# Probabilities times values for four query blocks per value matmul, with one probability tile per query block

## The chip, the cores and the metric

The kernel runs on one core of a Trainium2 chip. The metric is the time of one execution on the device, in microseconds (us). A kernel is timed by runs of the whole program, and its figure is the median of them. A profile is one further execution, recorded by the hardware; its own time and its span (first to last instruction) are given with it.

## The reference, cut to what matters

Two layers of a decoder trunk are computed for 1024 tokens with 16 learned tokens ahead of them. Each layer has three attention branches side by side: a forgetting attention (FoX, 8 heads of 64), a latent attention (MLA, 8 heads, 96 wide for the scores and 64 for the values) and a sliding-window attention. The first two are causal over the whole sequence, and their inner part is the one that the change touches:

```python
def block(args):                      # one block of 128 queries, all heads
    i, qi = args[0], args[1]
    s = jnp.einsum('bqhd,bkhd->bhqk', qi, k).astype(jnp.float32) * scale
    if log_cum is not None:           # FoX only: s += log_cum[query] - log_cum[key]
        ...
    mask = (kpos[None, :] <= qpos[:, None]) & key_ok[None, :]
    s = jnp.where(mask, s, NEG)
    p = jax.nn.softmax(s, axis=-1)
    return jnp.einsum('bhqk,bkhd->bqhd', p.astype(v.dtype), v)
```

All of it is in float32. Each branch is then gated, projected, merged with the other two through sigmoid gates, projected again and added to the layer's input.

## The kernel before, in words

**Precision.** A float32 product is made of fp32r matmuls: an operand is split into a high part and a low part, and high times high, high times low and low times high are added in PSUM. In `mm3` (lines 171 to 178) this is three matmuls of a projection (lines 175, 176, 177). In the values product it is done otherwise: the two parts of the values stand side by side as the 128 stationary columns of one weight tile (64 high, 64 low), so one weight tile meets the high part of the probabilities (line 310) and then the low part (line 312).

**Attention of one head.** The 16 learned tokens are a small block of their own; the 1024 tokens are 8 query blocks and 8 key blocks of 128. `softmax_of` makes the scores of one query block for all keys that it sees (144 columns for block 0, 1040 for block 7) in chunks of up to 512 columns (lines 802, 804 for FoX, line 1001 for MLA), VectorE adds the mask and takes the running minimum from PSUM into the probability tile `P` (line 255), ScalarE takes the exponential in place and the row sum (line 260), and GpSimd copies the 16 columns of the learned tokens out to `pmeta` (line 298). `P` is 1040 columns wide and comes from a ring of 5 buffers in FoX and 6 in MLA, `NP = (5, 6)`.

**Probabilities times values.** The probabilities must be turned so that keys lie on the partitions. `flipped` (lines 264 to 272) transposes up to four 128x128 blocks on TensorE into one PSUM tile `ps_t` (line 268), ScalarE copies the high part to `pth` (line 157), VectorE subtracts to get the low part `ptl` (line 158). `attention` works in groups of four query blocks with one PSUM tile `o` of 512 columns, but inside a group in two halves (`sub`) of two query blocks. Each half makes its two softmaxes, then walks the key blocks in pairs: a flip holds two key blocks for two query blocks (512 columns; on the diagonal three blocks, 384 columns), and each key block gets two matmuls (lines 310, 312) of 256 columns, or of 128 for the last key block on the diagonal. Then `halves` adds the two halves of the partitions of `o` into `u` (lines 280, 281), and the second half of the group begins. One head has 10 flips, 36 transposes and 40 values matmuls; there are 32 heads in all (2 layers, 2 branches, 8 heads).

**Values.** `load_v` (lines 393 to 402) fetches the values of a pair of heads with one DMA into `vraw`, which takes a buffer of the `P` ring, and GpSimd rounds them and subtracts (lines 391, 401) to fill `vp` (2 buffers).

**What orders the work.** The program is written against a scheduler that sets the order of every engine's instructions when the kernel is built: earlier in the program goes first, and what is not ready, by its model of time, is passed over by later work. Each buffer, and each PSUM bank, is guarded by semaphores as a whole. After every group `fill()` puts dense projections behind it as written in `PLAN` (gates, `z` columns, and in MLA columns of the first branch's projection), and through that the dense matmuls and the attention are mixed on TensorE. All DMAs are issued by SyncE (SP) from one queue, in order.

## Time and profile before

| | |
|---|---|
| median of 3 runs | 2570.98 us (2567.51 to 2572.38) |
| the profiled execution, its own time | 2569.85 us |
| its span, first to last instruction | 2567.8 us |
| granted TensorE clock, mean | 0.998 |
| VectorE busy | 1273.4 us (50%) |
| ScalarE busy | 1205.8 us (47%) |
| GpSimd busy | 1012.9 us (39%) |
| DMA, queue 1: packet time as a share of 16 engines' span | 38.0% |

In the rows of the profile PE is TensorE's matmul, PEld its weight load, DVE VectorE, ACT ScalarE, POOL GpSimd and SP SyncE. A row names the line, the engine, the operation, the output and its inputs by the program's names, and the shapes. [...] The stages of layer 0 lie in this order: FoX attention from about 300 to 600 us, the window attention to about 825, MLA to about 1090, then the merge; in layer 1 FoX from about 1580 to 1910, MLA from about 2090 to 2360.

### The profile page before, as it was taken

The page shows a single profiled execution, that of the slowest core. Times are in us where ns is not written, and L with a number is a line of the kernel's source. Part 1 is how long each engine was busy: PE and PEld are TensorE (multiplying, and loading weights), DVE is VectorE, ACT ScalarE, POOL GpSimd, SP SyncE. Part 2 cuts the span into 40 slices and gives each one's busy share as a digit, 9 for nine tenths or more (in the row PEclk, how much of TensorE's full clock was granted, in tenths as well). Part 3 has the DMA queues.
Part 4 walks back from the last instruction along what each step waited for, and adds up shares of the span by engine and source line. Part 5 has one row for each costly group of instructions (what it writes and reads, how often), then busy time and mean ns, then how long its engine had stood idle before and what let it go on. Part 6 is the DMA issues. An engine that isn't in the chain of part 4 may idle for free.

```text
span 2567.8 us, 42092 instructions
## 1 busy us (share of the span) xinstructions
PE 2517.1 (98%) x15446; PEld 2247.5 (88%) x15446; DVE 1273.4 (50%) x3279; ACT 1205.8 (47%) x2704; POOL 1012.9 (39%) x990
## 2 busy tenths in 40 slices
PE   8999999999999999999999999999999999999998
PEld 7999899999888999899998888888887888887797
DVE  6454355544363445657156463545434623565643
ACT  5234355545374556654233343555435634566433
POOL 2241545443332424463523325454423342353644
PEclk9999999999999999999999999999999999999999
DMA  5244512222634434364333353221326362453532
GB/s 170 62 136 150 189 54 82 73 78 77 172 105 115 129 101 126 102 228 166 114 90 99 97 198 138 66 88 56 98 69 176 100 169 81 124 146 115 183 130 74
DMA packets 137630, 303.39 MB, mean 118 GB/s; under 512 B 22560, under 2 KB 63296, under 8 KB 137424
## 3 DMA queue, kind: packets, MB, share of 16 engines
q1 hardware_dynamic: 137424, 300.71, 38.0%
q8 instruction: 122, 2.00, 0.3%
q14 instruction: 84, 0.69, 0.1%
HBM read 211.98 MB, written 88.66 MB: 117 GB/s over the span
## 4 chain that ended last, share of the span: by engine, by line
PE 79%; DMA 5%; DVE 2%; ACT 2%; POOL 2%; issue 1%; SPq 0%; POOLq 0%; ACTq 0%; DVEq 0%
PE ps_pj L175 14%; PE ps_pj L176 14%; PE ps_pj L177 14%; PE ps_t L268 5%; PE ps_s L1001 3%; PE ps_o L312 3%; PE ps_o L310 2%; PE ps_s L177 2%; PE ps_s L176 2%; PE ps_s L175 2%; PE ps_s L804 1%; PE ps_s L802 1%; PE ps_o L176 1%; PE ps_o L177 1%; PE ps_o L175 1%
## 5 line engine op out<-in xcount | busy, mean ns | idle before, releaser
L158 POOL TENSOR_TENSOR wl<-wr,wh 128x1024 fp32r<-128x1024 f32 (+1 forms) x156 | 376.1, 2411 | 776.7 <-ACT wh L157 653.5
L175 PE MATMUL ps_pj<-hh,wh 128*128 128x512 f32 (+1 forms) x1920 | 672.7, 350 | 3.5 <-ACT gt L657 2.0
L176 PE MATMUL ps_pj<-hl,wh 128*128 128x512 f32 (+1 forms) x1920 | 671.0, 349 | 0.0
L177 PE MATMUL ps_pj<-hh,wl 128*128 128x512 f32 (+1 forms) x1920 | 669.6, 349 | 0.9 <-POOL wl L158 0.9
L175 PEld LDWEIGHTS ps_pj<-hh,wh 128*128 128x128 f32 x1920 | 361.3, 188 | 46.7 <-ACT gt L657 2.6
L177 PEld LDWEIGHTS ps_pj<-hh,wl 128*128 128x128 f32 x1920 | 361.5, 188 | 42.3 <-POOL wl L158 1.1
L176 PEld LDWEIGHTS ps_pj<-hl,wh 128*128 128x128 f32 x1920 | 361.4, 188 | 39.4 <-issue 0.5
L158 DVE TENSOR_TENSOR ptl<-ps_t,pth 128x512 fp32r<-128x512 f32 (+1 forms) x386 | 244.5, 640 | 143.6 <-ACT pth L157 137.8
L260 ACT ACTIVATE P<-P,mn 128x656 f32<-128x656 f32 (+8 forms) x272 | 207.0, 761 | 165.1 <-DVE mn L255 160.5
L157 ACT CAST pth<-ps_t 128x512 fp32r<-128x512 f32 (+1 forms) x386 | 205.7, 546 | 165.3 <-PE ps_t L268 131.9
L157 ACT CAST wh<-wr 128x1024 fp32r<-128x1024 f32 (+1 forms) x156 | 162.1, 1039 | 237.0 <-PE ps_pj L176 134.5
L268 PE MATMUL ps_t<-ident,P 128*128 128x128 f32 x1152 | 186.2, 275 | 0.8 <-DVE ptl L158 0.7
L310 PE MATMUL ps_o<-pth,vp 128*128 128x256 f32 (+1 forms) x640 | 167.2, 277 | 2.7 <-DVE u L281 1.7
L312 PE MATMUL ps_o<-ptl,vp 128*128 128x256 f32 (+1 forms) x640 | 159.4, 287 | 2.7 <-DVE ptl L158 2.5
L298 POOL COPY pmeta<-P 128x16 f32<-128x16 f32 x256 | 49.3, 196 | 270.1 <-ACT P L260 261.9
L1001 PE MATMUL ps_s<-kt,qt 96*128 96x328 f32 (+9 forms) x696 | 146.4, 327 | 2.7 <-DVE mn L255 2.6
L268 PEld LDWEIGHTS ps_t<-ident,P 128*128 128x128 f32 x1152 | 134.2, 140 | 8.6 <-DVE ptl L158 1.5
L310 PEld LDWEIGHTS ps_o<-pth,vp 128*128 128x128 f32 x640 | 120.6, 189 | 11.2 <-ACT pth L157 1.7
L809 POOL TENSOR_TENSOR cm<-ckb,tri 128x128 f32<-128x128 f32 (+1 forms) x136 | 60.3, 445 | 175.2 <-DVE mn L255 171.4
L312 PEld LDWEIGHTS ps_o<-ptl,vp 128*128 128x128 f32 x640 | 120.6, 188 | 9.6 <-DVE ptl L158 5.6
L281 DVE TENSOR_TENSOR u<-ps_o,hv 64x256 f32<-64x256 f32 x128 | 53.9, 421 | 135.4 <-ACT hv L280 120.2
L1001 PEld LDWEIGHTS ps_s<-kt,qt 96*128 96x128 f32 (+1 forms) x696 | 108.0, 186 | 10.1 <-DVE mn L255 5.2
(354 smaller groups left out, 5641.7 us busy)
## 6 DMA issues: line engine op xcount, KB each, us to landing
wr<-in_w_dram SPq DMA_DIRECT2D x108, 512.0 KB
gate_d<-gt SPq DMA_DIRECT2D x72, 256.0 KB
gt<-gate_d SPq DMA_DIRECT2D x24, 520.0 KB
wr<-in_wbr_dram SPq DMA_DIRECT2D x24, 512.0 KB
gt<-gate_d SPq DMA_DIRECT2D x24, 512.0 KB
kn_d<-sg SPq DMA_DIRECT2D x16, 520.0 KB
ckb<-ck_d SPq DMA_DIRECT2D x16, 520.0 KB
kt<-kn_d SPq DMA_DIRECT2D x16, 520.0 KB
```

What stands on the lines that cost most here:

```text
L157: nc.scalar.copy(hi, src)
L158: (eng or nc.vector).tensor_tensor(lo, src, _f(hi), ALU.subtract)
L175: nc.tensor.matmul(dst, w1, rh[:, k, c0:c1], start=(k == 0), stop=False)
L176: nc.tensor.matmul(dst, w1, rl[:, k, c0:c1], start=False, stop=False)
L177: nc.tensor.matmul(dst, wl[:, k * P:k * P + m], rh[:, k, c0:c1], start=False, stop=(k == nk - 1))
L260: nc.scalar.activation(s[:rows, :n], s[:rows, :n], AF.Exp, bias=prev, scale=-1.0, accum_out=total)
L268: nc.tensor.transpose(t[:kk, c:c + rows], src, ident[:rows, :rows])
L281: nc.vector.tensor_tensor(u[mine, :n], o[mine, :n], t[mine, :n], ALU.add)
L310: nc.tensor.matmul(dst, vp[:, j + x, vs], ph[:, cols], start=(j + x == 0), stop=False)
L312: nc.tensor.matmul(dst, vp[:, j + x, vs], pl[:, cols], start=False, stop=(diag and x == 1))
L809: nc.gpsimd.tensor_tensor(cm[:rows, :rows], ckb[:rows, d:n], tri[:rows, :rows], ALU.add)
L1001: nc.tensor.matmul(dst, q[:, qi, q0:q0 + rows], kt[:, ki, c0:c1], start=(x == 0), stop=(x == 2))
```

## The change

A group's four softmaxes are made first. Then the key blocks are walked one by one: a flip holds one key block for all of the group's query blocks that see it (four blocks, 512 columns, up to the first diagonal block; then three, 384 columns; the last two key blocks, with two blocks and one, share a flip of 384). Each key block gets two matmuls as wide as that: 512, 384, 256 or 128 columns. `halves` for both halves of the group comes at the end. A head still has 10 flips and 36 transposes; values matmuls are 24 where they were 40.

The ring of `P` tiles gives way to one tile for each query block, each as wide as its block needs (144, 272, ... 1040 columns, one buffer each; the learned tokens' own block shares the first). `vraw` gets a buffer of its own of 512 columns, and `load_v` fills it twice, for four key blocks each time.

```diff
-    def softmax(pool, bufs, rows, n, qk, segs, total):
-        s = pool.tile([P, L], F32, tag="P", name="P", bufs=bufs)
+    def softmax(pool, rows, n, qk, segs, total):
+        width = max(n, NM + P)
+        s = pool.tile([P, width], F32, tag=f"P{width}", name="P", bufs=1)
...
             o = psum("o")
-            for sub in range(2):
-                i0 = 4 * g + 2 * sub
-                pt = [softmax_of(i, sums[:, hb * 8 + i:hb * 8 + i + 1]) for i in (i0, i0 + 1)]
-                oo = o[:, 256 * sub:256 * sub + 256]
-                for b in range(2):
-                    nc.gpsimd.tensor_copy(pmeta[:, i0 + b, ms], pt[b][:, 0:NM])
-                for j in range(0, i0 + 2, 2):
-                    k0 = NM + j * P
-                    diag = j == i0
-                    blocks = [(0, 0, 0), (1, 0, P), (1, 1, 2 * P)] if diag else \
-                        [(0, 0, 0), (1, 0, P), (0, 1, 2 * P), (1, 1, 3 * P)]
-                    width = 384 if diag else 512
-                    ph, pl = flipped(pool, [(pt[b][:, k0 + x * P:k0 + x * P + P], c, P)
-                                            for b, x, c in blocks], width)
-                    for x in range(2):
-                        cols = slice(256, 384) if diag and x else slice(256 * x, 256 * x + 256)
-                        dst = oo[:, 128:256] if diag and x else oo
-                        nc.tensor.matmul(dst, vp[:, j + x, vs], ph[:, cols], start=(j + x == 0),
-                                         stop=False)
-                        nc.tensor.matmul(dst, vp[:, j + x, vs], pl[:, cols], start=False,
-                                         stop=(diag and x == 1))
-                halves(pool, oo, u[:, NM + i0 * P:NM + i0 * P + 256], hb, 256)
+            i0 = 4 * g
+            pt = [softmax_of(i, sums[:, hb * 8 + i:hb * 8 + i + 1]) for i in range(i0, i0 + 4)]
+            for b in range(4):
+                nc.gpsimd.tensor_copy(pmeta[:, i0 + b, ms], pt[b][:, 0:NM])
+            for js in [[j] for j in range(i0 + 2)] + [[i0 + 2, i0 + 3]]:
+                items, parts, c = [], [], 0
+                for j in js:
+                    b0, k0, at = max(0, j - i0), NM + j * P, c
+                    for b in range(b0, 4):
+                        items.append((pt[b][:, k0:k0 + P], c, P))
+                        c += P
+                    parts.append((j, slice(at, c), o[:, P * b0:]))
+                ph, pl = flipped(pool, items, c)
+                for j, cols, dst in parts:
+                    nc.tensor.matmul(dst, vp[:, j, vs], ph[:, cols], start=(j == 0), stop=False)
+                    nc.tensor.matmul(dst, vp[:, j, vs], pl[:, cols], start=False, stop=(j == i0 + 3))
+            for c in (0, 256):
+                x0 = NM + i0 * P + c
+                halves(pool, o[:, c:c + 256], u[:, x0:x0 + 256], hb, 256)
             fill()
...
-    def load_v(pool, bufs, which, pair):
-        raw = pool.tile([P, L], F32, tag="P", name="vraw", bufs=bufs)
-        raw = raw[:, :NB * P].rearrange("p (t h c) -> p t h c", t=NB, h=2)
-        dma(raw, v_d[which][pair // 2][:, :, P * (pair % 2):P * (pair % 2) + P]
-            .rearrange("p t (h c) -> p t h c", h=2))
         vp = pool.tile([P, NB, 256], F32R, tag="vp", name="vp", bufs=2)
         v = vp.rearrange("p t (h e c) -> p t h e c", h=2, e=2)
-        rounded(v[:, :, :, 0], raw)
-        nc.gpsimd.tensor_tensor(v[:, :, :, 1], raw, _f(v[:, :, :, 0]), ALU.subtract)
+        for t in (0, NB // 2):
+            ts = slice(t, t + NB // 2)
+            raw = pool.tile([P, 512], F32, tag="vraw", name="vraw", bufs=1)
+            raw = raw.rearrange("p (t h c) -> p t h c", t=NB // 2, h=2)
+            dma(raw, v_d[which][pair // 2][:, ts, P * (pair % 2):P * (pair % 2) + P]
+                .rearrange("p t (h c) -> p t h c", h=2))
+            rounded(v[:, ts, :, 0], raw)
+            nc.gpsimd.tensor_tensor(v[:, ts, :, 1], raw, _f(v[:, ts, :, 0]), ALU.subtract)
         return vp
```

The callers lose the argument `NP[...]`; nothing else changes.

## The prediction

> **What bounds the kernel now.** I read the page's first two parts, then the chain of work that ended last, then the busy times of chosen stretches, and last the starts of single matmuls.

> ```profile
> span 2567.8 us, 42092 instructions
> PE 2517.1 (98%) x15446; PEld 2247.5 (88%) x15446; DVE 1273.4 (50%) x3279; ACT 1205.8 (47%) x2704; POOL 1012.9 (39%) x990
> PE 79%; DMA 5%; DVE 2%; ACT 2%; POOL 2%; issue 1%; SPq 0%; POOLq 0%; ACTq 0%; DVEq 0%
> ```

> TensorE is busy 98% of the span and carries 79% of the chain; no other engine exceeds half. So the first question is how many nanoseconds of TensorE's queue the change takes away. The second is where TensorE isn't covered, because there a shorter queue buys nothing and a longer wait costs. The stretches of full-sequence attention (columns: stretch, its length, then busy us of PE, PEld, DVE, ACT, POOL with instructions in brackets):

> ```profile
> 300.00:600.00 300.00, 299.23 (x2050) 277.39 (x2048) 151.80 (x499) 153.61 (x344) 145.07 (x192) 1.00 0.22 71
> 827.00:1000.00 173.00, 170.97 (x1193) 160.38 (x1194) 81.38 (x236) 91.38 (x208) 55.61 (x67) 1.00 0.43 115
> 1580.00:1910.00 330.00, 330.00 (x1879) 287.92 (x1878) 157.48 (x508) 161.85 (x326) 141.45 (x180) 1.00 0.23 74
> 2100.00:2203.00 103.00, 103.00 (x557) 89.14 (x557) 34.29 (x97) 41.32 (x83) 29.63 (x33) 1.00 0.40 112
> 2300.00:2358.00 58.00, 57.00 (x349) 50.40 (x348) 37.21 (x92) 36.59 (x75) 11.91 (x17) 1.00 0.31 98
> ```

> ```profile
> 1000.00:1045.00 45.00, 43.25 (x305) 39.71 (x305) 31.00 (x93) 32.12 (x78) 28.47 (x39) 1.00 0.53 157
> 2203.00:2300.00 97.00, 92.57 (x587) 81.12 (x586) 64.87 (x176) 62.56 (x134) 53.18 (x57) 1.00 0.52 133
> ```

> In the first five, TensorE never rests for more than a few us in all: the dense projections that `fill()` supplies cover every wait of the attention. The last two are thin stretches of MLA, where the attention runs nearly alone; DVE and ACT are busy two thirds of the time there, and TensorE idles 1.75 and 4.43 us. Over all seven the idle time is 0.77 + 2.03 + 0 + 0 + 1.00 + 1.75 + 4.43 = 10.0 us: the most that better overlap could give back there.

> **The values matmuls.** Ten flips a head stay ten, with the same widths (six of 512, four of 384) and 36 transposes; so ScalarE's and VectorE's copies stay as they are. The columns streamed stay the same too: before, 2 x (6 x 512 + 4 x 384) = 9216 a head, after, 12 x 512 + 4 x 384 + 4 x 256 + 4 x 128 = 9216. What changes is into how many instructions they are cut: 40 before (32 of 256, 8 of 128), 24 after. The groups confirm the first:

> ```profile
> L310 PE MATMUL ps_o<-pth,vp 128*128 128x256 f32 x512 | 140.2, 290 | 2.7 <-DVE u L281 1.7 <-ACT pth L157 0.9
> L312 PE MATMUL ps_o<-ptl,vp 128*128 128x256 f32 x512 | 137.3, 290 | 2.7 <-DVE ptl L158 2.5
> L312 PE MATMUL ps_o<-ptl,vp 128*128 128x128 f32 x128 | 35.2, 275 | 0.0
> L310 PE MATMUL ps_o<-pth,vp 128*128 128x128 f32 x128 | 28.5, 223 | 0.0
> ```

> Their means (290 and some 250 ns) overlap each other, so they are no prices. The price of one is the distance of starts in an unbroken row (columns: start, duration, engine, line, operation; xN merges N):

> ```profile
> 700.95 0.39 PE L175 MATMUL ps_pj<-hh,wh 128*128 128x512 f32 x1
> ...
> 706.27 0.40 PE L177 MATMUL ps_pj<-hh,wl 128*128 128x512 f32 x1
> ```

> ```profile
> 1011.10 0.28 PE L310 MATMUL ps_o<-pth,vp 128*128 128x256 f32 x1
> ...
> 1012.04 0.49 PE L268 MATMUL ps_t<-ident,P 128*128 128x128 f32 x3
> ...
> 1014.61 0.22 PE L310 MATMUL ps_o<-pth,vp 128*128 128x128 f32 x1
> 1014.66 0.28 PE L312 MATMUL ps_o<-ptl,vp 128*128 128x128 f32 x1
> 1014.78 0.30 PE L268 MATMUL ps_t<-ident,P 128*128 128x128 f32 x1
> ```

> ```profile
> 1017.33 0.87 PE L1001 MATMUL ps_s<-kt,qt 96*128 96x392 f32 x4
> 1018.04 0.28 PE L175 MATMUL ps_pj<-y,wh 128*128 128x264 f32 x1
> ```

> From the first to the last of 24 dense matmuls of 512 columns are 23 steps in 5.32 us, 231.3 ns each. Eight values matmuls of 256 take 0.94 us, 117.5 ns each. A high and low pair of 128 takes 0.17 us. Four of 392 take 0.71 us, 177.5 ns; I scale that to 174 ns for 384. So a column costs about 0.45 ns, and below 256 columns more: the pair of 128 takes 170 ns for 256 columns, where one matmul of 256 takes 117.5.

> Before, a head costs 32 x 117.5 + 4 x 170 = 4440 ns. After, 12 x 231.3 + 4 x 174 + 4 x 117.5 + 2 x 170 = 4282 ns. The difference is 158 ns a head and, over 32 heads, **5.1 us**. The weak term is the 256, of which 28 a head fall away: each nanosecond on it moves the sum by 28 x 32 ns = 0.9 us. The row of eight is rounded to 10 ns, so 1.25 ns either way: 4.0 to 6.2 us. Nearly all stretches above are ones where TensorE is the bound, so I count the sum as time on the path.

> [...]

> **The waits inside a group.** Before, the second half of a group writes into the PSUM bank that the first half's `halves` is still reading, so its first L310 waits for L281: 1.7 us in the group's row above. That wait goes. After the hi-matmul the lo-matmul waits for `ptl` as before (2.5 us in its row): the same number of flips, the same copies. I take 0.9 us for the first, half of what is shown, since the flips behind it have to be reached by VectorE anyway.

> **Four softmaxes before the first product.** This wait is added. Product 0 of a group needs the exponentials of all four query blocks. Behind it on TensorE's queue stand the other flips of the group; VectorE and ScalarE have the flips' copies queued after the last reduction and exponential. What covers it: the products of the group before, which read four other `P` tiles (one for each query block, so eight in all, against five or six in the ring, one of which `vraw` takes at times), and the fill. Where the fill is gone, in the thin stretches, it costs up to the second pair of exponentials per group. One such and its read:

> ```profile
> 2348.55 1.17 ACT L260 ACTIVATE P<-P,mn 128x1040 f32<-128x1040 f32 x1 [0.32 <-DVE mn L255]
> 2349.62 0.19 ACT L260 ACTIVATION_READ_ACCUMULATOR P<-P,mn 128x1 f32 x1
> ...
> 2357.87 0.27 ACT L333 ACTIVATE rt<-ps_t 16x128 f32<-16x128 f32 x1 [1.29 <-PE ps_t L331]
> ```

> ```profile
> 1000.00:1045.00 45.00, 10.51 (x39) 7.36 (x39) 1.00 0.53 157
> 2203.00:2300.00 97.00, 20.71 (x76) 14.22 (x76) 1.00 0.52 133
> ```

> The second fence is L310 alone in the thin stretches: 115 of them at 20 a head, so 5.75 heads or 11.5 groups. Two exponentials of the widest kind with their reads are 2.72 us, so the bound is 31 us; the other bound is below nothing, because the deeper set of tiles may remove part of the 6.2 us of idle time there. I take 0: the group before has 10 or 26 transposes and 8 or 16 products left when these exponentials run.

> At MLA's end in layer 1 (third row above) the last exponential and its read are over by 2349.8 and the row sums are turned at 2357.9: 8 us in which four flips remained. After, seven remain. But the exponentials will come earlier, since no flip stands among them. I take 0, with minus 2 to plus 3 us as its ends.

> **The values loaded in halves.** One more DMA per pair of heads, and the second must wait until GpSimd has read the first. Behind it on SP stand the next head's keys and queries, and the weights for the fill. The tightest place is MLA's start in layer 0:

> ```profile
> 811.30 0.56 SPq L101 DMA_DIRECT2D vraw<-v_d  x1
> 811.91 0.66 SPq L101 DMA_DIRECT2D kt<-kn_d  x1
> ```

> ```profile
> 817.09 2.77 POOL L391 TENSOR_SCALAR vp<-vraw 128x1024 fp32r<-128x1024 f32 x1 [11.80 <-DMA vraw<-v_d]
> 822.19 2.40 POOL L401 TENSOR_TENSOR vp<-vraw,vp 128x1024 fp32r<-128x1024 f32 x1
> ```

> ```profile
> 838.41 0.28 PE L310 MATMUL ps_o<-pth,vp 128*128 128x256 f32 x1
> ```

> From issue to GpSimd's start 5.8 us pass, and the two halves of its work are about 2.6 us each. So the values would be whole some 2 x (5.8 + 2.6) = 17 us after the issue, at 828, and the first product is at 838.4: covered by 10 us. If SP stands for the 8.4 us, the keys behind it slip by as much; the scheduler can put them ahead, and the fill covers the rest (170.97 of 173 us busy from 827 on). I take 0, with 0 to 4 us, half of such a slip at one place without cover. GpSimd's work is the same number of elements in twice the instructions, on an engine that is busy 39%.

> **The sum** is 5.1 + 0.9 = 6.0 us off the profiled execution's 2569.85 us, of which 2567.8 are span and 2.05 lie around it: 2563.9. The median of the runs shown is 1.13 us above the profiled one, so on that footing the forecast is 2570.98 - 6.0 = **2565.0 us**. A measurement of this kernel can tell about 0.2%, that is 5.1 us, from no change: the runs before span 0.19%.

> **The rivals.**

> *Only the equal cuts pay.* Two 256s cost 235 ns and one 512 costs 231.3, so 12 such merges give 44 ns a head. The other 114 ns rest on a 384 costing 174 and not 117.5 + 85 as its parts. If the extra cost of a narrow matmul is that of its neighbour's weight load and moves elsewhere, only 32 x 44 = 1.4 us remain: 2569.6, no change. Against it: the row of 392. [...]

> *Thin stretches grow.* In the 11.5 groups where the fill is used up TensorE waits for the second pair's exponentials. For it: DVE and ACT at two thirds there, and the `P` of block 7 is free only after the group's last flip, so the next head's block 7 can't start before. Against it: the cover named above, and the 0.9 us in all for which L310 waited for ACT in its row above. At half of 31 us it is plus 15.5 - 5.1 = 10 us: 2581. It eats the saving at 16% of the bound and shows as slower from 33% on.

> *The overlap gets better as well.* Eight tiles and no stop inside a group take back part or all of the 10.0 us of idle time in the attention. With half of it, 2570.98 - 5.1 - 5.0 = 2560.9; with all, 2555.9. For it: 6.2 of the 10.0 us lie where copies and not fill set the pace. Against it: those copies stay as many.

> **How the numbers follow.** The forecast 0.45, only equal cuts 0.15, thin stretches grow 0.20, better overlap 0.20. The forecast's 6.0 us lie just past the 5.1 that can be told, and the ends of its terms lie on both sides of that; I give 0.29 of its 0.45 to faster and 0.16 to no change. So faster is 0.29 + 0.20 = 0.49, no change 0.16 + 0.15 = 0.31, slower 0.20. The range goes from 2556 (all idle time back) to 2579 (13 of the 31 us exposed, 13 - 5 above the median before); what is left out is the worse part of the thin stretches. As the signs are mixed: the forecast's own range is 2561 (6.2 + 1.7 + 2 off) to 2574 (4.0 off, 3 for the tail and 4 for the load on).

> **What would show it.** In the profile after: values groups with x384 of 512 columns and x128 each of 384, 256 and 128 over both lines; starts 231 ns apart for 512 and near 174 for 384; PE busy in FoX's stretches still whole; L310 no longer released by L281; idle time between 1000 and 1045 and between 2203 and 2300 as before (6 us). The forecast is wrong if the 384 steps are near 200 ns, if TensorE idles more than some 5 us longer in MLA, or if the chain of waits names `vraw`, the keys or ScalarE's exponentials ahead of L310.

## The result, and the profile after

The changed kernel takes 2604.9 us (median of 4 runs, 2600.98 to 2609.39) where the kernel before takes 2571.68 us (4 runs, 2567.51 to 2575.63): a ratio of 1.0125, with a 95% interval of 1.0112 to 1.0138. It is **slower by 33 us**, where 2565.0 was forecast with a range of 2556 to 2579, and on the side that had 0.20. The profiled execution took 2609.39 us, 4.5 above its median; its span is 2607.6 us and its mean granted clock 0.990 (before: 2567.8 us and 0.998). The page after begins:

```profile
span 2607.6 us, 40940 instructions
PE 2534.9 (97%) x14934; PEld 2233.4 (86%) x14934; DVE 1271.4 (49%) x3279; ACT 1201.2 (46%) x2704; POOL 1020.9 (39%) x1022
```

512 matmuls are gone (15446 to 14934, 16 for each of 32 heads), and yet TensorE is busy for 17.8 us *longer*, and it idles longer too. I cut both programs into ten stages, at the same places of the program (value projection, FoX, window attention, MLA, merge, in each layer; before, the window attention of layer 0 begins at 660 us and not near 600). Shown are the value projection of layer 0, the window attention of both layers, MLA of layer 1, and the sum of all ten (columns as in the prediction: PE's busy time comes first, PEclk is the third value from the right). After:

```profile
32.00:320.00 288.00, 278.30 (x1765) 253.16 (x1765) 146.43 (x266) 104.05 (x230) 90.04 (x65) 1.00 0.39 127
...
680.00:842.00 162.00, 156.09 (x1007) 139.25 (x1005) 83.60 (x297) 88.90 (x271) 45.86 (x26) 0.98 0.43 116
...
1968.00:2124.00 156.00, 149.12 (x756) 124.01 (x756) 73.46 (x264) 82.89 (x238) 41.92 (x23) 0.98 0.43 118
2124.00:2501.00 377.00, 363.08 (x1823) 300.19 (x1822) 204.28 (x456) 190.05 (x389) 163.02 (x157) 0.99 0.45 135
...
sum 2564.00, PE 2511.36 PEld 2211.75 DVE 1250.75 ACT 1177.48 POOL 997.76; mean PE 251.14 PEld 221.17 DVE 125.08 ACT 117.75 POOL 99.78
```

Before:

```profile
31.00:314.00 283.00, 277.95 (x1768) 253.34 (x1767) 146.92 (x269) 104.07 (x230) 84.89 (x59) 1.00 0.40 129
...
660.00:826.00 166.00, 163.16 (x1066) 145.02 (x1065) 82.65 (x302) 91.06 (x274) 48.98 (x25) 1.00 0.45 121
...
1935.00:2092.00 157.00, 154.34 (x792) 127.36 (x791) 79.18 (x264) 84.56 (x239) 47.86 (x24) 1.00 0.46 130
2092.00:2460.00 368.00, 357.76 (x1949) 304.98 (x1948) 201.94 (x453) 189.65 (x387) 158.01 (x148) 1.00 0.46 135
...
sum 2525.00, PE 2494.07 PEld 2226.32 DVE 1253.09 ACT 1182.62 POOL 989.77; mean PE 249.41 PEld 222.63 DVE 125.31 ACT 118.26 POOL 98.98
```

The ten stages are 2564 - 2525 = 39.0 us longer; the two profiled executions lie 39.5 us apart, 6 us more than the medians, so this ledger is theirs. Of the 39.0 us, idle time is (2564 - 2511.36) - (2525 - 2494.07) = 52.6 - 30.9 = **21.7 us**, and busy time 2511.36 - 2494.07 = 17.3 us. The idle time grew by 4.7 us in the value projection, 3.1 and 4.2 in the window attention and 3.7 in MLA of layer 1. The busy time needs another view, the granted clock. In stretches of 50 us the clock after is below 1.00 in these eight between 300 and 2300 us; before, it is 1.00 in every stretch from 50 to 2550 us:

```profile
300.00:350.00 50.00, 44.49 (x272) 39.91 (x271) 17.02 (x58) 17.00 (x38) 30.48 (x32) 0.93 0.18 59
650.00:700.00 50.00, 46.26 (x282) 40.55 (x281) 13.35 (x45) 17.96 (x50) 20.10 (x16) 0.93 0.75 187
800.00:850.00 50.00, 47.30 (x292) 42.49 (x292) 11.16 (x37) 17.01 (x43) 16.98 (x11) 0.97 0.54 139
1000.00:1050.00 50.00, 44.97 (x261) 38.57 (x261) 30.38 (x89) 31.95 (x76) 22.80 (x32) 0.93 0.47 126
1600.00:1650.00 50.00, 50.00 (x262) 42.91 (x263) 24.63 (x84) 22.67 (x48) 28.19 (x36) 0.97 0.17 56
1700.00:1750.00 50.00, 48.59 (x248) 40.75 (x247) 23.09 (x74) 25.16 (x50) 29.41 (x31) 0.97 0.25 85
1950.00:2000.00 50.00, 45.24 (x227) 37.77 (x227) 22.91 (x85) 27.12 (x80) 21.39 (x17) 0.93 0.76 192
2250.00:2300.00 50.00, 45.27 (x237) 37.75 (x238) 27.49 (x79) 27.48 (x60) 22.54 (x28) 0.93 0.42 116
```

That is (5 x 0.07 + 3 x 0.03) x 50 = **22.0 us** of clock withheld. Not all of it lengthened the work: in three slices of 3.4 us at half clock (the first two stand in rows further on) TensorE was busy for only 1.50, 1.99 and 2.14 us, so half of their 4.6 us of idle time, some 2.3 us, was withheld while nothing ran. That leaves an estimated 19.7 us of lower clock, and 17.3 us of added busy time were found. So the ledger reads: 21.7 of new idle time, 19.7 of lower clock, and some 2.4 saved where the prediction took 5.1. As the ends of matmuls are modelled, it can't be read much finer.

The instructions are cut as foretold. The groups of line 307 (it was 310) have the counts of the prediction, and in an unbroken row of FoX the starts stand 230 and 240 ns apart for 512 columns and 180 ns for 384 (the prediction had 231.3 and 174):

```profile
L307 PE MATMUL ps_o<-pth,vp 128*128 128x512 f32 x192 | 80.0, 417 | 5.6 <-ACT pth L156 5.5
...
L307 PE MATMUL ps_o<-pth,vp 128*128 128x384 f32 x64 | 22.6, 352 | 0.0
```

```profile
1708.09 0.39 PE L307 MATMUL ps_o<-pth,vp 128*128 128x512 f32 x1
1708.32 0.40 PE L308 MATMUL ps_o<-ptl,vp 128*128 128x512 f32 x1
1708.56 0.34 PE L307 MATMUL ps_o<-pth,vp 128*128 128x384 f32 x1
1708.74 0.49 PE L268 MATMUL ps_t<-ident,P 128*128 128x128 f32 x3
```

The wait on L281 is gone as well. The first L307 row above names what stands in its place: L307 waits 5.5 us for `pth`, where L310 waited 0.9.

**One hole from close by.** FoX starts with a hole, a time without work for TensorE, of 4.92 us. GpSimd's row at that place after, then SyncE's, then TensorE's:

```profile
307.98 1.49 POOL L388 TENSOR_SCALAR vp<-vraw 128x512 fp32r<-128x512 f32 x1
...
313.57 1.49 POOL L388 TENSOR_SCALAR vp<-vraw 128x512 fp32r<-128x512 f32 x1 [2.73 <-DMA vraw<-v_d]
315.14 1.26 POOL L400 TENSOR_TENSOR vp<-vraw,vp 128x512 fp32r<-128x512 f32 x1
316.36 2.34 POOL L157 TENSOR_TENSOR wl<-wr,wh 128x1024 fp32r<-128x1024 f32 x1
318.78 1.81 POOL L780 TENSOR_SCALAR qq<-qq 64x264 fp32r<-64x264 f32 x2
```

```profile
310.86 5.93 SPq L100 DMA_DIRECT2D vraw<-v_d  x2
```

```profile
319.70 0.19 PE L801 MATMUL ps_s<-ks,qq 128*16 128x16 f32 x1 [4.92 <-POOL qq L780]
...
321.20 0.63 PE L176 MATMUL ps_pj<-hh,wl 128*128 128x512 f32 x1
...
323.76 0.63 PE L176 MATMUL ps_pj<-hh,wl 128*128 128x512 f32 x1
```

GpSimd stands 2.73 us for a half of the values, SyncE's row of two issues spans 5.93 us, and behind those values on GpSimd's queue stands the rounding of the first queries, `qq`, which TensorE needs for FoX's first scores. Before, that was done at 310.5:

```profile
310.53 1.88 POOL L781 TENSOR_SCALAR qq<-qq 64x264 fp32r<-64x264 f32 x2
```

When TensorE is released, six dense matmuls of 512 columns take from 321.20 to 323.76, 427 ns each, where they took 231.3. Cut into slices of 3.4 us, after shows why this is counted as clock and not as waiting:

```profile
314.40:317.80 3.40, 0.38 (x4) 0.16 (x2) 0.00 (x0) 0.38 (x1) 3.32 (x3) 1.00 0.04 11
317.80:321.20 3.40, 1.50 (x6) 1.31 (x7) 0.59 (x4) 0.79 (x3) 3.08 (x4) 0.50 0.66 203
321.20:324.60 3.40, 3.40 (x9) 2.64 (x8) 0.91 (x5) 0.51 (x2) 2.51 (x5) 0.50 0.04 17
324.60:328.00 3.40, 3.40 (x16) 2.75 (x15) 0.00 (x0) 0.14 (x1) 0.00 (x0) 0.99 0.00 0
```

The two slices in which TensorE works for 0.38 and 1.50 us are each *followed* by one at half clock (0.50); the full slice 321.20 to 324.60 is followed by full clock. So this hole is paid while it lasts, and in part again behind it: the slice from 321.20 is full, and half of its 3.4 us, 1.7 us, is lost.

### The profile page after: what moved, and what is told of

It is laid out like the page before. It is cut to its first block, busy times and chain, and to the rows that moved or that the text cites. A ratio compares the mean times of both kernels' runs of the same rounds, so it can differ in the third digit from the quotient of the medians.

```text
span 2607.6 us, 40940 instructions
## 1 busy us (share of the span) xinstructions
PE 2534.9 (97%) x14934; PEld 2233.4 (86%) x14934; DVE 1271.4 (49%) x3279; ACT 1201.2 (46%) x2704; POOL 1020.9 (39%) x1022
## 5 line engine op out<-in xcount | busy, mean ns | idle before, releaser
L175 PE MATMUL ps_pj<-hl,wh 128*128 128x512 f32 (+1 forms) x1920 | 673.3, 351 | 0.0
L157 POOL TENSOR_TENSOR wl<-wr,wh 128x1024 fp32r<-128x1024 f32 (+1 forms) x156 | 376.1, 2411 | 719.6 <-ACT wh L156 645.8
L175 PEld LDWEIGHTS ps_pj<-hl,wh 128*128 128x128 f32 x1920 | 364.2, 190 | 41.9 <-issue 0.5
L157 DVE TENSOR_TENSOR ptl<-ps_t,pth 128x512 fp32r<-128x512 f32 (+1 forms) x386 | 241.7, 640 | 188.6 <-ACT pth L156 186.2
L260 ACT ACTIVATE P<-P,mn 128x656 f32<-128x656 f32 (+8 forms) x272 | 207.0, 761 | 197.6 <-DVE mn L255 195.7
L268 PE MATMUL ps_t<-ident,P 128*128 128x128 f32 x1152 | 188.9, 275 | 0.5 <-ACT P L260 0.5
L268 PEld LDWEIGHTS ps_t<-ident,P 128*128 128x128 f32 x1152 | 145.1, 142 | 23.9 <-issue 0.8
L1000 PE MATMUL ps_s<-kt,qt 96*128 96x328 f32 (+9 forms) x696 | 151.7, 331 | 4.6 <-DMA qt<-qr_d 2.7
L308 PE MATMUL ps_o<-ptl,vp 128*128 128x512 f32 (+3 forms) x384 | 137.2, 376 | 4.4 <-DVE ptl L157 4.1
L307 PE MATMUL ps_o<-pth,vp 128*128 128x512 f32 (+3 forms) x384 | 134.9, 353 | 6.2 <-ACT pth L156 5.5
L255 DVE CUSTOM_DVE_ANT_0 P<-ps_s,mz 128x144 f32<-128x144 f32 (+7 forms) x128 | 62.5, 493 | 107.4 <-PE ps_s L1000 68.5
L255 DVE CUSTOM_DVE_ANT_0 P<-ps_s,ckb 128x16 f32<-128x16 f32 (+7 forms) x128 | 56.2, 443 | 109.7 <-PE ps_s L803 76.8
L307 PEld LDWEIGHTS ps_o<-pth,vp 128*128 128x128 f32 x384 | 73.2, 191 | 16.6 <-ACT pth L156 8.8
```

The lines of the kernel that those rows point to most:

```text
L157: (eng or nc.vector).tensor_tensor(lo, src, _f(hi), ALU.subtract)
L175: nc.tensor.matmul(dst, w1, rl[:, k, c0:c1], start=False, stop=False)
L255: nc.vector.tensor_tensor_reduce(s[:rows, x0:x1], t[:rows, x0 - c0:x1 - c0], b[:, x0 - s0:x1 - s0], 1.0, prev, ALU.add, ALU.min, mn[:rows, ...
L260: nc.scalar.activation(s[:rows, :n], s[:rows, :n], AF.Exp, bias=prev, scale=-1.0, accum_out=total)
L268: nc.tensor.transpose(t[:kk, c:c + rows], src, ident[:rows, :rows])
L307: nc.tensor.matmul(dst, vp[:, j, vs], ph[:, cols], start=(j == 0), stop=False)
```

## The experiments

Each kernel below ran beside the kernel before on the same chip, whose median there was 2572.5 to 2573.5 us. Theory A blames the values' load that now runs ahead, theory B the long row of softmaxes ahead of the products.

**The change taken apart.** The first four put back or add one part. In the first, the changed kernel's values come by one DMA into query block 7's tile; in the second, as halves into that tile. The edit of the second:

```diff
-            raw = pool.tile([P, 512], F32, tag="vraw", name="vraw", bufs=1)
+            raw = pool.tile([P, L], F32, tag="P1040", name="vraw", bufs=1)[:, :512]
```

> The changed kernel, but its values come by one DMA again, into the tile of query block 7 (1040 columns), so that a pair's load can't start before that tile is free; the loop and the eight tiles stay. Theory A (the load is at fault: with a buffer of its own it runs ahead into the starts of FOX and MLA, and its halves make SP and GpSimd wait for each other; in the changed kernel TensorE idles some 9 us at those three starts and then loses some 7 us to half clock): 12 to 16 us come back, 2589 to 2593 us. Theory B (the loop is at fault: four softmaxes before the first product and the flips in a row behind them leave holes in the thin stretches of MLA): nothing comes back, 2600 to 2610 us.

> The changed kernel, values in halves, but both halves go into the tile of query block 7 and not into a buffer of their own. Theory A in the form that the own buffer is what lets the loads run ahead: like the run with one DMA, 2589 to 2593 us. Theory A in the form that the halves are what hurts: like the changed kernel or worse, 2600 to 2612 us. Theory B: 2600 to 2610 us.

Measured: 2634.09 us (1.0237, 1.0222 to 1.0252) and 2659.38 us (1.0328, 1.031 to 1.0345). Both are slower than the change itself and outside the figures of both theories. Values that share a tile with a query block wait for its last flip, and its softmax waits for them: in the first TensorE waits 8.0 us for `vp` ahead of its products, in the changed kernel no such wait shows. That tests another wait and not the one removed. The second differs from the change in the tile alone, so a buffer of its own is the better home for the values.

The third is the kernel before with one tile for each query block, the old loop, and the load at once into block 7's tile; the fourth is the kernel before with the new loop only, in the ring of 5 and 6.

> The kernel before with one probability tile per query block in place of the ring, the values loaded at once into block 7's tile; its loop with two query blocks at a time stays. Theory A and theory B: within 6 us of the kernel before, 2566 to 2578 us, since neither the load nor the loop is changed. Theory C (single tiles hold up the next head's softmaxes): over 2585 us.

> The kernel before with the new loop alone: four softmaxes first, matmuls of up to 512 columns; the ring of 5 and 6 tiles stays, and values are loaded at once into a buffer of the ring. A group holds four tiles of the ring, so only one or two are left for softmaxes ahead. Theory B: as slow as the changed kernel or slower, 2600 to 2640 us, holes in every thin stretch. Theory A: under 2590 us, since the load is as before.

Measured: 2595.61 us (1.0091, 1.0076 to 1.0106) and 2657.84 us (1.0328, 1.0313 to 1.0344). Both lie above what theories A and B gave. The fourth is slower than the change by 53 us: the loop does badly in the ring, where a group of four holds nearly all of the buffers. The third fits theory C by its number, but it has the shared tile in it and so doesn't price the tiles; the tenth does, and speaks against theory C.

**Undo the loop, hold the load.** The fifth is the changed kernel with the old loop over halves of a group.

> The changed kernel with the old loop (two query blocks, then two more): the eight tiles and the values' own buffer, filled by halves, stay. Theory A (the load's collisions at the starts of FOX and MLA, with the half clock that follows them, are some 14 us) together with theory B (the loop costs the rest): 2578 to 2590 us. Theory A alone: no change from the changed kernel, 2600 to 2610. Theory B alone: as the kernel before, 2567 to 2576.

Measured: 2583.05 us (1.0045, 1.003 to 1.006), as theories A and B together had it. So the loop costs about 22 of the 33 us, and tiles and load the rest. The seventh is the changed kernel with the next pair's load held back until the pair before has made its fifth query block:

```diff
+            if hold is not None and t == 0:
+                nc.gpsimd.tensor_copy(raw[:, 0:1], hold[:, 4, 0:1])   # hold: pmeta of the pair before
```

> The changed kernel, but a pair's values (from the second pair on) may be loaded only after the pair before has made its first head's fifth softmax: a copy of one column into the buffer holds the DMA. Nothing of pair 1 can then run at FOX's start. Theory A: the hole of 5.2 us at FOX's start of layer 0 and the 2.1 us of layer 1 go, and with them three or four windows of half clock: 10 to 14 us less, 2591 to 2595 us. If the collisions cost nothing: 2600 to 2610 us.

Measured: 2598.19 us (1.01, 1.0085 to 1.0115), 7 us off and not 10 to 14. The tenth joins the two:

> The changed kernel with the old loop over pairs of query blocks, and the next pair's value load held back: what is left of the change is one tile per query block and the halves in a buffer of their own. Theory A (all that the tiles and the halves cost is the load that runs ahead into FOX's start: a hole of 5.2 us, 6.8 us at half clock behind it, 8.6 us together): 2571 to 2577, level with the kernel before, which stood at 2573. Rival (the tiles themselves cost it): 2580 to 2585, no change against the run with the load not held.

Measured: 2571.52 us against 2572.54, a ratio of 0.9994 (0.9985 to 1.0003). Theory A holds for this part: tiles and halves cost nothing that can be told once the load doesn't run ahead. The hole at FoX's start is gone with its half clock; the same two slices of this kernel:

```profile
314.40:317.80 3.40, 3.40 (x20) 2.83 (x18) 1.57 (x8) 1.54 (x6) 2.42 (x5) 1.00 0.00 0
317.80:321.20 3.40, 3.40 (x19) 2.91 (x18) 0.43 (x3) 1.08 (x3) 0.55 (x2) 1.00 0.00 0
```

From this base the loop alone costs 2598.19 - 2571.52 = **26.7 us**, saving of its matmuls included.

**Where the loop loses.** The thirteenth and fourteenth have the held load and the new loop in one branch only.

> The changed kernel with the load held, the new loop in FOX's attention and the old one in MLA's. Theory B (the new loop loses in each branch, at its own place: by the stages' lengths of the held runs with the new and the old loop, 6.4 and 8.5 us in FOX with the sliding-window stage behind it, 4.1 and 8.1 in MLA): 2571.5 + 15 = 2586, so 2583 to 2590. Rival (one branch pays and the other loses all): at or under 2572 if FOX is the one that pays, 2595 to 2600 if it is the one that loses.

> The same with the new loop in MLA's attention and the old one in FOX's. Theory B: 2571.5 + 12 = 2584, so 2580 to 2588. Rival (one branch pays): at or under 2572, or 2595 to 2600.

Measured: 2583.96 us (1.0041, 1.0029 to 1.0053) and 2585.93 us (1.0043, 1.0027 to 1.0059). Over the tenth that is 12.4 and 14.4 us, together 26.8: the loop loses in both branches, and the two losses add up to the whole, as theory B had it. For FoX most of it lies in the first 20 us of the window attention behind it. Layer 1, with the new loop in FoX, in MLA, and in neither (the tenth):

```profile
1947.00:1967.00 20.00, 14.97 (x74) 12.05 (x73) 11.91 (x50) 13.50 (x47) 5.62 (x3) 0.83 1.04 252
```

```profile
1939.00:1959.00 20.00, 18.40 (x88) 13.84 (x87) 6.87 (x27) 6.63 (x19) 5.44 (x3) 1.00 1.04 261
```

```profile
1931.00:1951.00 20.00, 18.69 (x91) 14.19 (x90) 6.62 (x26) 7.00 (x19) 6.12 (x3) 1.00 1.04 264
```

With the new loop in FoX TensorE idles 5.0 us there in place of 1.3, and the clock is 0.83, another 3.4 us withheld; the DMA share of 1.04 in all three says that the window attention's loads run then, but with the old loop in FoX TensorE still has other work: 63 and 61 matmuls of dense projections (lines 174 to 176) run there in the tenth and the fourteenth, and 18 in the thirteenth. Layer 0 shows the same, less strongly, with the new loop in FoX and in neither:

```profile
672.00:692.00 20.00, 15.07 (x86) 12.53 (x87) 4.81 (x28) 5.61 (x25) 7.12 (x4) 0.91 1.04 219
```

```profile
662.00:682.00 20.00, 17.16 (x112) 14.45 (x113) 9.00 (x28) 7.68 (x25) 10.01 (x5) 1.00 1.04 255
```

Added idle time and withheld clock come to 3.7 + 3.4 = 7.1 us in layer 1 and 2.1 + 1.8 = 3.9 in layer 0, together 11.0 of the 12.4 us. In MLA the flips wait. The waits of TensorE in MLA of layer 1, after and before:

```profile
PE ps_o L307 <- ACT pth L156: 4.7, 5, 2.0
```

```profile
PE ps_o L310 <- ACT pth L157: 0.6, 2, 0.4
```

One of them, in ScalarE's row after: the flip's cast stands behind a gate (`gt`, read back from memory) whose DMA is late, and TensorE has nothing else, since the next product needs that flip.

```profile
2283.39 1.15 ACT L950 ACTIVATE gt<-gt 128x512 f32<-128x512 f32 x2 [2.00 <-DMA gt<-gate_d]
2284.45 0.56 ACT L156 CAST pth<-ps_t 128x512 fp32r<-128x512 f32 x1
```

A second of the five is alike; the two are 3.5 of the 4.7 us. With the new loop in MLA alone the longest of these waits, 3.2 us, has a gate ahead of it too. For the exponentials themselves (`P`) TensorE waits only 0.5 us in all of the changed kernel. So what shows in MLA is ScalarE's queue held up by a transfer at a moment when TensorE has nothing else; no run here loads the gates earlier.

**Softmaxes earlier.** If the row of softmaxes ahead of the products is to blame, making it overlap with other products should help. The sixth makes all eight softmaxes of a head ahead of its products; the ninth does that with the load held; the twelfth, load held, puts two of the second group's four ahead.

> The changed kernel with all eight softmaxes of a head written ahead of its first product, so that the second group's are made while the first group's products run. Theory B in the form that a group's products wait for its own four softmaxes: the thin stretches of MLA lose most of their added holes and half clock, some 20 us, 2580 to 2590 us. Theory B in the form that the row of seven flips itself is what can't be covered: no change, 2600 to 2612 us, since the flips then come later still.

> The changed kernel with both repairs: all eight softmaxes of a head emitted before its products, and the next pair's value load held back. Theory A+B (late load and long serial row, each its own holes): the gains add, 9 us and 7 us off 2605, so 2587 to 2592, with no half-clock slice at FOX's start in either layer. Rival (both repairs fill the same holes): no better than the better of them alone, 2594 to 2600. If the order of the built program is what moves the time, anything between 2575 and 2615.

> The changed kernel with the load held and, ahead of the first group's products, two of the second group's four softmaxes. Theory B (the row of softmaxes ahead of the products leaves TensorE alone, and the thin products at a head's end leave the others alone; spreading them helps): at or under the run with all eight ahead, 2582 to 2592. Rival (the eight ahead gain only by being ahead of everything): between the held load alone and that, 2592 to 2599.

Measured: 2595.62 us (1.0089, 1.0068 to 1.0111), 2585.17 (1.0052, 1.0033 to 1.007) and 2590.73 (1.0072, 1.0058 to 1.0086). The sixth falls between the two figures that were put down for it. The two repairs at least add up, as the ninth's first theory said: 9.3 and 6.7 us alone, 19.7 together, a little more than was forecast. The twelfth lies in theory B's range by its number, but between the held load and the ninth, as its rival said, and not level with the ninth: from the held load's 2598.19, two ahead take off 7.5 us and all eight 13.0. Half of the loop's 26.7 us therefore hangs on when the softmaxes come. The first 20 us of layer 1's window attention in the ninth (a profiled execution 7.9 us above its median) are nearly whole again; only the clock is not:

```profile
1949.00:1969.00 20.00, 18.15 (x84) 14.59 (x83) 7.32 (x27) 8.57 (x26) 5.95 (x3) 0.91 1.03 262
```

The other half, 13.7 us over the tenth, is not brought back by any kernel here.

**A control for depth.** The eleventh is the kernel before with `NP = (5, 5)`: one probability tile fewer in MLA.

> A control: the kernel before with a ring of five probability tiles in MLA in place of six, nothing else. Theory (the depth that a head's four softmaxes had in MLA was not the limit): 2570 to 2580, clock 0.996 or more. If the kernel before stands on a knife's edge, where any other order of the program opens holes and brings the half clock, 2585 to 2620 with a clock of 0.985 to 0.993, and then the order itself, not the wide products, is to blame for much of the loss.

Measured: 2584.3 us (1.0045, 1.0028 to 1.0062). I had expected 2570 to 2580, and that was wrong: one buffer costs 12 us with the old loop. The stretch of MLA around 1000 us, in this kernel and in the kernel before:

```profile
995.00:1060.00 65.00, 60.76 (x388) 53.74 (x388) 44.37 (x126) 44.12 (x106) 38.46 (x50) 0.92 0.45 124
```

```profile
995.00:1060.00 65.00, 62.72 (x451) 58.01 (x451) 46.55 (x134) 46.84 (x113) 46.92 (x59) 1.00 0.47 135
```

Idle time grows from 2.3 to 4.2 us and, with it, 0.08 x 65 = 5.2 us of clock are withheld. One reading is that the time of MLA's thin stretches hangs on how far the softmaxes run ahead of the products already with the old loop. The other was put down before the run: any other order of the program opens holes, which would give 2585 to 2620. The measured time lies just below that. The tenth, in another order again, loses nothing, so not every order does; but how much of the loop's loss is the order that was built, and not the wide products themselves, no run here separates.

**The price of a hole.** The eighth fills the holes at the window attention's start with 24 useless matmuls in each layer.

> The changed kernel with 24 useless matmuls of 512 columns (5.5 us) ahead of the window attention's first scores in each layer, where TensorE idles some 4.5 us while it waits for queries and then has 6.8 us of half clock. Theory H (half clock follows a 3.4 us window of which TensorE idles over about half): the windows of half clock at 683 and 1973 us vanish; the added 5.5 us lie in the holes, so the time is 2 x 3 us less or the same: 2597 to 2606 us. If the clock has another cause: 2 x 5.5 us more, 2612 to 2618 us, and the windows stay.

Measured: 2614.84 us (1.0166, 1.0151 to 1.0181), 10 us over the change. The 48 useless matmuls are 48 x 231.3 ns = 11.1 us of work. The clock from 1950 to 2000 us rose from 0.93 to 1.00, as the theory of the half clock has it, but the time is that of the other theory, and in MLA of layer 1 the granted clock was still 0.98 from 2100 to 2500 us. Nothing was won in the sum: inconclusive for the price.

The last four are the kernel before with stops of TensorE made on purpose in the output projection: a copy by VectorE between transposes (many short, few long), then VectorE's rewriting of the products' own operand (short, long).

```diff
+                t = psum("t")
+                for c in (0, P):
+                    nc.tensor.transpose(t[:, c:c + P], ident, ident)
+                x = po.tile([P, 256], F32, tag="hole", name="hole", bufs=1)
+                for _ in range(6):                                   # 1 for the short ones
+                    nc.vector.tensor_copy(x, t[:, :256])
+                nc.tensor.transpose(t[:, :P], x[:, :P], ident)
```

> The kernel before with useless work that stops TensorE on purpose, in the output projection of both layers, where it is otherwise never idle: ahead of each of some 36 blocks of columns two transposes, one copy of their result by VectorE, and a transpose of the copy. A hole is about 0.9 us (0.43 us of copy and two handovers), 32 us together. Both theories of the half clock: no slice under 1.00 in that stage, and the time 2572 plus the sum of the holes as the trace shows them, about 2605.

> The same with a third of the holes, each about three times as long (six copies one after the other, 3.0 us; some 12 of them, 36 us together). If a hole that empties more than half of a 3.4 us slice brings a slice at half clock behind it: 8 to 11 such slices in the stage, 1.7 us lost by each, so 2572 plus the holes' sum plus 13 to 19, about 2620 to 2627. If a hole costs its length only: 2572 plus the holes' sum, about 2608.

```diff
+                for _ in range(2):                                   # once, columns 0:4, for the short ones
+                    for e0, e1 in och:
+                        x = mt[e0][1][:, 0, :]
+                        nc.vector.tensor_tensor(x, _f(x), _f(x), ALU.max)
```

> The kernel before, in the output projection of both layers: ahead of each of some 36 blocks of columns VectorE rewrites four columns of each block's low part in place (three short operations, values unchanged), which every product after it needs and every product before it reads, so TensorE stands for their length and two handovers, about 0.7 us, 25 us together. Both theories: no slice at half clock in that stage, and the time 2573 plus the sum of the holes as the trace has them.

> The same ahead of each third block only, with the whole first slab of the low part rewritten twice: about 3.1 us of VectorE and the handovers, some 12 holes of 3.6 us, 43 us together. If a hole that empties more than half of a 3.4 us slice brings a slice at half clock: 10 to 14 such slices in the stage, 1.7 us lost in each, so 2573 plus the sum of the holes plus 16 to 24. If a hole costs its length only: 2573 plus the sum of the holes, and no such slice.

Measured: 2596.52 us (1.0084, 1.0064 to 1.0104), 2577.65 (1.0013, 1.0003 to 1.0024), 2575.22 (0.9999, 0.9987 to 1.0012) and 2572.83 (0.9997, 0.9985 to 1.001). Only the first lost much, if less than the 2605 put down for it, and the two long ones missed both of their figures: none of the four made the holes that were meant, since when the kernel is built the scheduler puts other blocks' products into their place. In the sixteenth the transposes ahead of the copies begin at 1205.3 and those behind them only at 1214.7:

```profile
L1052 PE MATMUL ps_t<-ident x12: 271/272/272, 1205.3 to 1263.5; 128*128 128x128 f32 x12
L1056 PE MATMUL ps_t<-ident,hole x6: 270/270/273, 1214.7 to 1270.1; 128*128 128x128 f32 x6
```

So what a hole costs beside its length was not measured by itself. What these runs show is the cover. The output projection of layer 0 in the eighteenth and before:

```profile
1206.00:1320.00 114.00, 113.95 (x730) 105.36 (x729) 74.54 (x119) 41.18 (x79) 56.15 (x37) 1.00 0.40 136
```

```profile
1204.00:1318.00 114.00, 114.00 (x732) 105.64 (x731) 43.43 (x87) 40.97 (x78) 53.01 (x37) 1.00 0.40 130
```

VectorE works 74.54 us in place of 43.43 there, on the products' own operand, and TensorE loses nothing, as long as other products can go first.

## Why the prediction was wrong

- **The matmuls.** Right in the counts and in the distances of starts. The 5.1 us themselves were not seen: the ledger leaves some 2.4 us for them, and every kernel with the new loop is slower, so no run shows the saving by itself.
- **The waits inside a group.** The wait on L281 went as said (0.9 us taken). "The same number of flips, the same copies" was true, but the order was not the same: the wait for `ptl` rose from 2.5 to 4.1 us in all, and the one for `pth` from 0.9 to 5.5 us.
- **"Four softmaxes before the first product... I take 0."** Wrong, and the step that failed: with the load held the loop costs 26.7 us, which with the 5.1 forecast as saved makes some 32 us. The argument was that "the group before has 10 or 26 transposes and 8 or 16 products left". It looked at TensorE's supply within a head and not at the edges of a stage: FoX's last group is followed by loads into memory that FoX frees, and the whole row of softmaxes and flips comes ahead of them. FoX was booked as fully covered from stretches that stop at 600 and 1910 us, short of its end, and 12.4 us were lost through it. For MLA the rival "thin stretches grow" named the branch, as one place of two. That its 2581 lies near the 2585.9 measured with the loop in MLA alone is in part luck: it had TensorE wait for exponentials, and the waits shown are those for the flips' casts behind a gate's DMA.
- **"The values loaded in halves... I take 0, with 0 to 4 us."** Wrong as well, in place and size. I checked MLA's start in layer 0, and only whether the *first* product would have its values. The loss is at FoX's start, from the next pair's load, and through GpSimd's queue: what waits behind a value half is the rounding of queries. The text said "Behind it on SP stand the next head's keys and queries", and did not ask the same of GpSimd. With the old loop it costs 2583.05 - 2571.52 = 11.5 us, with the new one 2604.9 - 2598.19 = 6.7 us.
- **The clock.** Nothing was said of it, since before its body shows 1.00 throughout. The 22.0 us of withheld clock are as much as the added idle time, so a forecast of waiting had to allow for the clock too. What one hole costs beside its length was not measured by itself.
- **What is shown and what isn't.** Shown: tiles and halves are level with before once the load is held; the loop loses in both branches, and half of that comes back when softmaxes are made earlier. That the FoX part is due to the released memory, and that the gates' loads are to blame in MLA, is read from the traces, not tried. The other 13.7 us of the loop were not brought back and stay open, and so does the share of the built order in them. No kernel here beats the one before.

## What to carry to other kernels

Where TensorE is busy 98% and a part is to save 5 us of 2570, look at the edges of each stage, where cover ends, and ask for each queue (GpSimd's and ScalarE's too) what stands behind an instruction that now waits. Batching more producers ahead of one wide consumer lengthened, here, the row that nothing covers at a stage's end; making them earlier brought half of it back. The transfer that got a buffer of its own started earlier: the second pair's values, in layer 0, were issued from 304.19 us on, where before they were issued at 378.18. Say when such a transfer should start.

## What the runs showed of the hardware

```profile
679.60:683.00 3.40, 1.76 (x12) 1.39 (x12) 0.29 (x1) 0.39 (x1) 3.40 (x2) 1.00 1.03 223
683.00:686.40 3.40, 1.99 (x10) 1.94 (x11) 0.39 (x4) 0.69 (x4) 3.01 (x2) 0.51 1.04 228
```

TensorE is busy 1.76 of 3.40 us by the profile, in twelve matmuls, and the next slice has 0.51. Cut into slices of 3.413 us in step with those starts, from 30 us after the start on, the traces before and after have 4 slices at full clock in which TensorE is busy for less than 45%, and all 4 are followed by half clock; of the 1438 that are busy for 75% or more none is. Between the two some are and some aren't (5 of 8 from 45 to 55%, 3 of 29 from 55 to 75%), and why is not settled by these runs.
